# Read-back sums enter the PSUM banks by products with the identity at the end of a mixture of experts

## The chip, the cores and the metric

The kernel runs on one core of a Trainium2 chip. The metric is the device time of one execution in microseconds (us), as the median of several runs. The engines are TensorE (PE, with its weight loads shown apart as PEld), VectorE (DVE), ScalarE (ACT), GpSimd (POOL) and SyncE (SP, which issues most DMA transfers). TensorE writes into eight PSUM banks of 128 partitions by 512 f32 values.

## What is computed

A two-layer backbone block over 256 latent tokens and 256 context tokens of width 1024. Each layer mixes the tokens by four head groups, and then a mixture of 16 experts (two for each token) is added with a gate:

```python
def moe_ffn(h, w_router, router_bias, w_gate, w_up, w_down):
    ...
    y = jnp.zeros_like(h)
    for e in range(N_EXPERTS):
        a = jax.nn.silu(h @ w_gate[e]) * (h @ w_up[e])
        y = y + gates[..., e:e + 1] * (a @ w_down[e])
    return y
...
x = x_mid + g2 * moe_ffn(hf, ...)        # latent tokens
ctx = ctx_mid + cg2 * moe_ffn(hc, ...)   # context tokens, first layer only
```

So in the first layer 512 tokens, held as four tiles of 128 tokens by 1024, each receive gate vector times sum of expert outputs. After it the second layer starts with an RMSNorm of the same tiles.

## The kernel before

**Turns.** In the first layer `moe` runs 16 turns, one for each expert (`turn_0`, in the order `TURNS`). A turn gathers the expert's tokens in blocks of 64, multiplies them with the gate and up weights (`mm_in`, line 1544), forms silu times product with the token's weight (`act`, lines 1550 and 1551), transposes (`spin`, line 1557) and multiplies with the down weights (`mm_out`, line 1568). If the expert has more than 64 tokens, a second block runs in a branch (`If cv > BLK`), and inside it another branch (line 1760) covers a third block.

**Where the outputs go.** The first 15 experts add their rows to a table `sums` in device memory by indirect DMA (`put`, line 1451). At the end of turn 14 (`p == NE - 2`) the table is read back into four tiles `ACC` (line 1813); three of them lie over constants in the tile `cst`, which are loaded again later (line 531). In the same turn the gate vectors of latent and context tokens are spread over all partitions into `g2` (the tiles `G`). The last expert doesn't use the table. `parts` (lines 1586 on ACT and 1587 on DVE) splits each of its two output blocks into a rounded half and a rest, in `more` for the second block and `ST[0]` for the first, and `add` (line 1597) spreads them over the tokens by products with one-hot matrices, two such products for each bank, one bank for each half of a token tile. With `last` set DVE multiplies the bank by `g2` (line 1602), and DVE or POOL adds it to the residual tile `xres` (line 1603).

**The scaling before.** `scaled` multiplies each `ACC` tile by `g2` (line 1724) and adds it to `xres` (line 1725), tile 0 on DVE, tile 1's product on DVE and its sum on POOL, tiles 2 and 3 on POOL. It is called in the last turn between the first block's `act` and the second `mm_out`.

**Order.** Inside the turns PE, DVE and ACT execute in written order (a manual schedule). In the next layer's mixer (`mix(1)`) only PE's order is written out; a planner places the other engines' instructions, and it may put them into the end of the stage before: line 574, which computes the scale of the next layer's first norm, is an example. `stat` (lines 1840 and 1842, with 276 and 277) computes each tile's sum of squares for the next norm, whose first steps are lines 556 and 558 (DVE and ACT scale the tiles) and line 238 (PE transposes them).

**Banks.** `bank(tag)` takes a PSUM bank of a tag; there are one `tp`, one `md`, two `pj`, two `sc` and two `ob`. In the last turn `md` holds the second block's output and one `sc` the first block's.

**Matmul records.** An f32 product of 512 columns shows as two records in the trace, one whose operands are rounded to `fp32r` as one. The long convolution, whose rows stand below as a price, issues f32 products of 128x128 by 128x512:

```python
for f in (m, 2 + m):
    b = bank("sc")
    for tt in range(2):
        mm(b[:, :N], lhsT=C("df", tt * 512 + f * P, tt * 512 + (f + 1) * P),
           rhs=u[tt][:, :N], start=(tt == 0), stop=(tt == 1))
```

Of the kernel before, what the change touches and what calls it, by code (L numbers as in the profile page):

```python
# [14 lines left out]
OP = mybir.AluOpType  # L15
# [108 lines left out]
def hybrid_block_kernel(ctx: ExitStack, tc: tile.TileContext, xin, const, fconst, par, fpar, misc, fng,  # L124
                        ada, win, wout, exps, out, dump=None, upto=99):
    nc = tc.nc
# [10 lines left out]
    def bank(tag="tp"):  # L137
        return psp.tile([P, 512], F32, name="b_" + tag, tag=tag, bufs=BANKS[tag])
# [120 lines left out]
    def C(name, a=0, b=None):  # L259
        at, n = CONST[name]  # L260
        return cst[:, at + a:at + (n if b is None else b)]
# [5 lines left out]
    ident = C("ident")  # L267
# [100 lines left out]
    xres, norms = {}, []  # L368
# [1027 lines left out]
    def moe(l, cnt, idx, gc, pd, pk, rk, hx, h0, hp):  # L1396

        T = 4 if l == 0 else 2
        N = T * P
        S = N // L  # L1400
        V = nc.vector
        with ExitStack() as mctx:
            ep = mctx.enter_context(right(f"ep{l}"))
            ew = mctx.enter_context(right(f"ew{l}", 2))
            if l == 0:
# [5 lines left out]
                ACC = [cst[:, at + D * t:at + D * (t + 1)] for t in range(3)] + [ep.tile([P, D], F32, name="acc")]  # L1411
# [18 lines left out]
            b = bank()  # L1430
# [39 lines left out]
            if l == 0:  # L1470
# [7 lines left out]
                g2 = G  # L1478
# [100 lines left out]
            def parts(b, st):  # L1579

                if l:
                    V.tensor_mul(msc[:, :512], b, g2f)
                    b = msc[:, :512]
                for h in range(2):
                    a, o = slice(64 * h, 64 * h + 64), slice(64 - 64 * h, 128 - 64 * h)
                    nc.scalar.activation(st[h][a], b[a], AF.Copy)
                    V.tensor_tensor(st[h][o], b[a], st[h][a].bitcast(F32), op=OP.subtract)  # L1587
                return st

            def add(*blocks, only=None, last=False, banks=None):  # L1590

                for t in range(T) if only is None else only:
                    for h in range(2):
                        cs = slice(h * 512, (h + 1) * 512)
                        b = banks[h] if banks else bank("ob")
                        for i, (st, ohT) in enumerate(blocks):
                            nc.tensor.matmul(b, lhsT=ohT[:, t * P:(t + 1) * P], rhs=st[h],  # L1597
                                             start=(i == 0), stop=(i == len(blocks) - 1))
                        if last:
                            pool = h and t < T - 1  # L1600
                            y = AM[2] if pool and t % 2 == 0 else HE[1].rearrange("p k s -> p (k s)")[:, cs]
                            V.tensor_mul(y, b, g2[t // 2][:, cs])
                            (nc.gpsimd if pool else V).tensor_tensor(xres[t][:, cs], xres[t][:, cs], y, op=OP.add)
                        else:
                            y = xres[t] if l else ACC[t]
                            V.tensor_tensor(y[:, cs], b, y[:, cs], op=OP.add)  # L1606
# [70 lines left out]
            def turn_0(p, e, cv, w, b0):  # L1677

                start, last = p == 0, p == NE - 1
                h, nh = HE[p % 2], HE[(p + 1) % 2]  # L1680

                def prepare(q, part):

                    if q < NE:
                        turn(G[q % 2], 0, P, part=part, h=HE[q % 2])

                if start:
                    more = third()
                    b0 = mm_in(w, h0, between=lambda k: k > 2 and (next(more, None), next(more, None)))
                    b = bank("ob")  # L1690
# [5 lines left out]
                more = None, None  # L1696
                if last:
                    ST.append([ew.tile([P, 512], F32R, name=f"st{h}", tag="y") for h in range(2)])
                    owed = ST[0], OT[0]
                    more = ep.tile([P, 2, 512], F32R, name="stl", tag="HE0")  # L1700
                    more = [more[:, i] for i in range(2)]
# [3 lines left out]
                    more = more, OT[1]  # L1705
# [11 lines left out]
                    if not last:  # L1717
                        mm_in(nw, nh, b=b2, ks=ks)

                def scaled():  # L1720
                    if last:
                        for t in range(T):
                            eng = V if t == 0 else nc.gpsimd
                            (V if t < 2 else nc.gpsimd).tensor_tensor(ACC[t], ACC[t], g2[t // 2], op=OP.mult)
                            eng.tensor_tensor(xres[t], xres[t], ACC[t], op=OP.add)

                def first(steps):
                    if not start:
                        mm_in(w, h, b=b0, ks=range(HEAD, 8), between=lambda k: steps[k]() if k in steps else None)
                        act(b0, gc[:, 0, e:e + 1], AM[0])  # L1730
# [6 lines left out]
                def vector(c):  # L1737
                    if p == NE - 2:
                        for i in range(2):
                            nc.scalar.activation(g2[c][:, i * 512:(i + 1) * 512], bcast(mT[l][:, 5], i, c), AF.Copy)  # L1740

                with tc.If(cv > BLK, label=f"turn{p}") as branch:
                    tc.mark_branch_hint_location(f"third{p}", cv > P, engines=[ET.PE, ET.DVE, ET.Activation])
                    steps = {3: lambda: vector(0), 5: lambda: vector(1)}
                    b1 = mm_in(w, h[:, :, BLK:], tag="md", between=lambda k: steps[k]() if k in steps else None)
                    act(b1, gc[:, 1, e:e + 1], AM[1])
                    if last:
                        where(e, OT[1], C("slot", 1, 2))
                        where(e, OT[0], C("slot", 0, 1))
                    if start:  # L1750
                        spin(AM[1], AT[1])
                    first({4: lambda: spin(AM[1], AT[1])})
                    scaled()
                    steps = {1: lambda: prepare(p + 2, 0), 2: lambda: spin(AM[0], AT[0]),
                             3: lambda: (start and (prepare(1, 0), prepare(1, 1)), prepare(p + 2, 1))}
                    b1 = mm_out(w, AT[1], bank("md"), lambda f: steps[f]() if f in steps else None)
                    if last:
                        parts(b1, more[0])
                        mm_out(w, AT[0], out)
                        with tc.If(cv > P, label=f"third{p}"):  # L1760
                            add(more, last=True)
                            block(e, w, turn(X, 0, BLK, h=h0), g3[:, e:e + 1], C("slot", 2, 3), *temp, last=True)
                            with tc.If(cv > P + BLK):
                                overflow(e, w, cv, P + BLK, *temp, last=True)
                            zero(OT[1])
                        main.done(4)
                    else:
                        with tc.If(cv > P, label=f"third{p}") as branch2:
                            turn(X, 0, BLK, h=h0)
                            put(b1, rows[1][:, e:e + 1])  # L1770
                            b3 = mm_in(w, h0, tag="tp")
                            act(b3, g3[:, e:e + 1], AM[1])
                            head(0)
                            spin(AM[1], AT[1])
                            head(1)
                            put(mm_out(w, AT[1], bank("ob")), rows3[:, e:e + 1])
                            mm_out(w, AT[0], out)
                            with tc.If(cv > P + BLK):
                                overflow(e, w, cv, P + BLK, *temp)
                            main.done(4)  # L1780
                        with branch2.Else():
                            main.repeat()
                            put(b1, rows[1][:, e:e + 1])
                            head(0, 1)
                            mm_out(w, AT[0], out)
                with branch.Else():
                    first({4: lambda: vector(0), 6: lambda: vector(1)})
                    main.repeat()
                    if last:
                        where(e, OT[0], C("slot", 0, 1))  # L1790
                        where(e, OT[1], C("slot", 1, 2))
                    scaled()
                    if start:
                        spin(AM[0], AT[0])
                        mm_out(w, AT[0], out)
                        for q in (1, 2):
                            prepare(q, 0)
                            prepare(q, 1)
                        head(0, 1)
                    else:  # L1800
                        head(0)
                        prepare(p + 2, 0)
                        spin(AM[0], AT[0])
                        prepare(p + 2, 1)
                        head(1)
                        mm_out(w, AT[0], out)
# [11 lines left out]
                if not last:  # L1818
                    main.done(2)
                    return ncv, nw, b2  # L1820
                parts(out, ST[0])
                for t in range(T):
                    add(owed, more, only=[t], last=True)
                    if t:
                        stat(t - 1)
                stat(T - 1)
# [311 lines left out]
```

## Time and profile before

| | us |
|---|---|
| median of 3 runs | 1328.83 |
| lowest and highest | 1328.79 and 1328.98 |
| the profiled execution | 1331.17 |
| its span in the trace | 1329.1 |
| PE busy in the span | 1146.8 (86%) |
| DVE busy | 538.7 (41%) |
| ACT busy | 314.6 (24%) |
| POOL busy | 293.9 (22%) |

Busy shares are means over stages that have different limits; the stage of this change lies from about 795 to 830 us. Times in rows are microseconds from the start of the span unless ns is written. [...] A bracket with an arrow names how long the engine had been idle and what released it.

### The profile page before, as it was taken

How to read it: one execution, taken by the hardware profiler on the slowest of the kernel's cores; microseconds unless marked ns; L12 is line 12 of the kernel's file. 1: busy time of each engine (PE TensorE's matmuls, PEld its weight loads, DVE VectorE, ACT ScalarE, POOL GpSimd, SP SyncE). 2: the span in 40 equal slices, each digit the busy share in tenths (PEclk: the TensorE clock that was granted, in tenths of full speed). 3: DMA queues.
4: the chain of work that ended last, by engine and by line, in shares of the span. 5: the costliest groups of instructions: out<-in, count | busy, mean ns of one | idle time of the engine just before them, and what ended most of it. 6: DMA issues, size and time to landing. Idle time of an engine off the chain costs nothing. (4 is left out here: it accounts for less than half of the span.)

```text
span 1329.1 us, 16569 instructions
## 1 busy us (share of the span) xinstructions
PE 1146.8 (86%) x6205; PEld 644.2 (48%) x6205; DVE 538.7 (41%) x1070; ACT 314.6 (24%) x569; POOL 293.9 (22%) x238
## 2 busy tenths in 40 slices
PE   6799998888899789988898996878879699999995
PEld 2456565566588633323333333657669433343331
DVE  5431867325522641101011028496443535434444
ACT  2422233222312211111111114424333211111111
POOL 4432231322023312111112036543315000000000
PEclk9999998988789879989899996989869799998998
DMA  9485443412563689399999936120135399994971
GB/s 366 192 320 190 153 164 112 158 55 83 180 254 127 232 354 329 113 381 384 394 382 401 374 120 229 64 90 23 64 127 219 129 397 419 419 404 188 411 299 50
DMA packets 48559, 310.61 MB, mean 234 GB/s; under 512 B 6017, under 2 KB 6209, under 8 KB 14096
## 3 DMA queue, kind: packets, MB, share of 16 engines
q1 hardware_dynamic: 41936, 292.77, 56.4%
q0 software_dynamic: 6320, 15.27, 4.4%
q8 instruction: 91, 1.49, 0.4%
q14 instruction: 68, 0.56, 0.1%
q10 hardware_dynamic: 144, 0.52, 0.1%
HBM read 297.99 MB, written 12.32 MB: 233 GB/s over the span
## 5 line engine op out<-in xcount | busy, mean ns | idle before, releaser
L603 POOL TENSOR_TENSOR ws<-w,ws 128x1024 fp32r<-128x1024 f32 x50 | 121.3, 2439 | 218.2 <-ACT ws L602 200.8
L1544 PE MATMUL b_pj<-w,HE 128*64 128x512 f32 x416 | 107.6, 653 | 23.1 <-issue 20.8
L234 PE MATMUL b_pj<-hh,ws 128*128 128x512 f32 (+1 forms) x448 | 123.0, 364 | 1.1 <-POOL ws L603 1.1
L1568 PE MATMUL b_sc<-w,rows 128*64 128x512 f32 x448 | 103.7, 604 | 0.6 <-ACT rows L1558 0.6
L693 DVE SCALAR_TENSOR_TENSOR cacc<-gl,pr,cacc 128x512 f32<-128x512 f32 (+1 forms) x120 | 92.7, 772 | 2.6
L234 PEld LDWEIGHTS b_pj<-hh,ws 128*128 128x128 f32 x448 | 79.9, 199 | 21.0 <-issue 9.7
L234 PE MATMUL b_pj<-hl,ws 128*128 128x512 f32 (+1 forms) x224 | 78.8, 352 | 0.0
L1544 PEld LDWEIGHTS b_pj<-w,HE 128*64 128x64 f32 x416 | 34.1, 149 | 84.5 <-issue 82.3
L602 ACT ACTIVATE ws<-w 128x1024 fp32r<-128x1024 f32 x50 | 52.5, 1052 | 70.2 <-PE b_pj L234 44.6
L277 POOL TENSOR_TENSOR rf<-rf,half 128x1 f32<-128x1 f32 x2 | 1.1, 551 | 287.9 <-DVE rf L276 287.9
L1606 DVE TENSOR_TENSOR x<-b_ob,x 128x512 f32<-128x512 f32 x68 | 44.0, 687 | 43.4 <-PE b_ob L1597 43.3
L1451 POOL DMA_INDIRECT sums<-y,rws x19 | 29.8, 1566 | 135.6 <-DVE y L1450 116.4
L1568 PEld LDWEIGHTS b_sc<-w,rows 128*64 128x64 f32 x448 | 31.1, 138 | 58.3 <-issue 56.5
L1551 DVE SCALAR_TENSOR_TENSOR X<-X,gc,b_pj 64x512 f32<-64x512 f32 x16 | 12.1, 754 | 107.7 <-ACT X L1550 107.7
L234 PE MATMUL b_md<-w,sT 128*32 128x256 f32 x704 | 54.3, 434 | 1.3 <-DVE mT L313 1.3
L1544 PE MATMUL b_pj<-w,hf 128*64 128x512 f32 x224 | 53.9, 618 | 1.0 <-PEq L1920 0.6
L1544 PE MATMUL b_pj<-w,x 128*64 128x512 f32 x224 | 52.9, 601 | 1.0 <-PEq L1920 1.0
L1450 DVE COPY y<-b_sc 128x512 f32<-128x512 f32 x15 | 10.4, 692 | 96.5 <-PE b_sc L1568 50.3
L1597 PE MATMUL b_ob<-st,ohT 128*128 128x512 f32 x76 | 33.6, 511 | 16.6 <-DVE st L1587 9.9
L234 PEld LDWEIGHTS b_pj<-hl,ws 128*128 128x128 f32 x224 | 44.6, 199 | 5.4
L1550 ACT ACTIVATE X<-b_pj 64x512 f32<-64x512 f32 x16 | 9.4, 588 | 157.3 <-PE b_pj L1544 149.6
L1456 POOL DMA_INDIRECT G<-hbuf,idx x15 | 15.2, 1013 | 105.8 <-PE b_ob L1528 56.7
(475 smaller groups left out, 2062.8 us busy)
## 6 DMA issues: line engine op xcount, KB each, us to landing
w<-in_exps_dram SPq DMA_DIRECT2D x168, 1024.0 KB
w<-in_ada_dram SPq DMA_DIRECT2D x48, 1024.0 KB
w<-in_win_dram SPq DMA_DIRECT2D x16, 1024.0 KB
hold<-in_exps_dram SPq DMA_DIRECT2D x12, 1024.0 KB
w<-in_wout_dram SPq DMA_DIRECT2D x8, 1024.0 KB
hf<-in_exps_dram SPq DMA_DIRECT2D x6, 1024.0 KB
cst<-in_exps_dram SPq DMA_DIRECT2D x6, 1024.0 KB
pr<-in_par_dram SPq DMA_DIRECT2D x2, 1461.5 KB
```

The source lines that it names most:

```text
L234: nc.tensor.matmul(out_, lhsT=lhsT, rhs=rhs, **kw)
L602: nc.scalar.activation(wh[:, :n], src, AF.Copy)
L603: nc.gpsimd.tensor_tensor(wl[:, :n], src, wh[:, :n].bitcast(F32), op=OP.subtract)
L693: nc.vector.scalar_tensor_tensor(ac, gl[:, :, j:j + L], R("cvw", i * 31 + j, i * 31 + j + 1), ac, op0=OP.mult, op1=OP.add)
L1450: V.tensor_copy(y, b)
L1451: nc.gpsimd.indirect_dma_start(out=sums[:, :], out_offset=bass.IndirectOffsetOnAxis(ap=row, axis=0), in_=y, in_offset=None, bounds_check=1 ...
L1456: nc.gpsimd.indirect_dma_start(out=g, out_offset=None, in_=hbuf[:, :], in_offset=bass.IndirectOffsetOnAxis(ap=ix, axis=0), bounds_check=N ...
L1544: nc.tensor.matmul(b[64 * j:64 * j + 64], lhsT=x, rhs=w[k // 2][:, at:at + 512], start=(k == 0), stop=(k == 7), tile_position=(0, 64 * j))
L1551: V.scalar_tensor_tensor(a[64:], a[64:], gate[64:], b[64:], op0=OP.mult, op1=OP.mult)
L1568: nc.tensor.matmul(b[64 * j:64 * j + 64], lhsT=aT[:, f, :], rhs=w[4 + f // 2][:, at:at + 512], start=(f == 0), stop=(f == 3), tile_positio ...
L1597: nc.tensor.matmul(b, lhsT=ohT[:, t * P:(t + 1) * P], rhs=st[h], start=(i == 0), stop=(i == len(blocks) - 1))
L1606: V.tensor_tensor(y[:, cs], b, y[:, cs], op=OP.add)
```

## The change

The scaling and adding of the read-back sums (`scaled`, 8 operations) goes. Instead each bank of the last expert's sums is begun by a product of the identity with the matching half of `ACC`, which leaves the bank open, and the two one-hot products add to it; the existing multiplication by `g2` then scales both. Six of the eight banks are begun ahead of the first sum, in tags `ob`, `ob`, `pj`, `pj`, `sc`, `tp`; the last two, for tile 3, reuse the `ob` banks once DVE has read them.

```diff
-            def add(*blocks, only=None, last=False, banks=None):
+            def add(*blocks, only=None, last=False, banks=None, more=False):
...
                             nc.tensor.matmul(b, lhsT=ohT[:, t * P:(t + 1) * P], rhs=st[h],
-                                             start=(i == 0), stop=(i == len(blocks) - 1))
+                                             start=(i == 0 and not more), stop=(i == len(blocks) - 1))
...
-                def scaled():
-                    if last:
-                        for t in range(T):
-                            eng = V if t == 0 else nc.gpsimd
-                            (V if t < 2 else nc.gpsimd).tensor_tensor(ACC[t], ACC[t], g2[t // 2], op=OP.mult)
-                            eng.tensor_tensor(xres[t], xres[t], ACC[t], op=OP.add)
...
                     first({4: lambda: spin(AM[1], AT[1])})
-                    scaled()
...
                         where(e, OT[1], C("slot", 1, 2))
-                    scaled()
...
                 parts(out, ST[0])
+
+                def begun(i):
+
+                    b = bank(("ob", "ob", "pj", "pj", "sc", "tp", "ob", "ob")[i])
+                    nc.tensor.matmul(b, lhsT=ident, rhs=ACC[i // 2][:, i % 2 * 512:(i % 2 + 1) * 512], start=True, stop=False)
+                    return b
+
+                banks = [begun(i) for i in range(6)]
                 for t in range(T):
-                    add(owed, more, only=[t], last=True)
+                    add(owed, more, only=[t], last=True, banks=banks[2 * t:2 * t + 2] if t < 3 else [begun(6), begun(7)], more=True)
                     if t:
                         stat(t - 1)
                 stat(T - 1)
```

## Rows read from the trace of the kernel before

**Rows 1.** Windows: stretch, length, each engine's busy us (instructions), PEclk, DMA share, GB/s.
```profile
784.00:797.00 13.00, 11.16 (x56) 3.75 (x52) 4.61 (x6) 1.95 (x4) 5.91 (x7) 1.00 0.74 258
797.00:801.40 4.40, 4.31 (x22) 1.15 (x16) 4.37 (x3) 0.59 (x1) 4.40 (x2) 1.00 0.04 11
801.40:808.10 6.70, 0.00 (x0) 0.00 (x0) 5.25 (x7) 1.19 (x3) 6.70 (x4) 0.70 0.44 158
808.10:818.00 9.90, 8.66 (x16) 4.19 (x16) 8.95 (x16) 4.02 (x12) 6.26 (x10) 0.50 0.78 287
...
822.00:828.00 6.00, 5.76 (x24) 4.71 (x24) 4.09 (x10) 5.23 (x11) 0.62 (x1) 0.50 0.89 348
```
**Rows 2.** Timeline of PE: start, us, line, operation, tiles, shape, count.
```profile
787.57 0.50 PE L1575 MATMUL b_tp<-pdT,pick 16*128 16x512 f32 x1 [1.84 <-DVE ohT L1576]
...
797.71 3.60 PE L1568 MATMUL b_sc<-hold,rows 128*64 128x512 f32 x16
808.12 0.79 PE L1597 MATMUL b_ob<-st,ohT 128*128 128x512 f32 x1 [6.80 <-DVE st L1587]
808.71 0.63 PE L1597 MATMUL b_ob<-stl,ohT 128*128 128x512 f32 x1
...
821.85 0.45 PE L238 MATMUL b_pj<-cst,xs 128*128 128x128 f32 x1 [4.00 <-issue]
```
**Rows 3.** Timeline of DVE, with one row of ACT.
```profile
797.77 3.02 DVE L1724 TENSOR_TENSOR cst<-cst,G 128x1024 f32<-128x1024 f32 x1
...
802.69 0.59 ACT L1586 ACTIVATE st<-b_sc 64x512 fp32r<-64x512 f32 x1 [0.55 <-ACTq L1760]
803.59 3.76 DVE L574 SCALAR_TENSOR_TENSOR aT<-mT,msc 128x4 f32<-128x4 f32 x4 [0.72 <-DVEq L1760]
807.38 0.69 DVE L1587 TENSOR_TENSOR st<-b_sc,st 64x512 fp32r<-64x512 f32 x1
808.72 0.69 DVE L1587 TENSOR_TENSOR st<-b_sc,st 64x512 fp32r<-64x512 f32 x1 [0.66 <-ACT st L1586]
809.44 0.69 DVE L1602 TENSOR_TENSOR HE<-b_ob,G 128x512 f32<-128x512 f32 x1
...
819.11 0.69 DVE L1603 TENSOR_TENSOR x<-x,HE 128x512 f32<-128x512 f32 x1
```
**Rows 4.** Line 574, whole trace: count, ns min/median/max.
```profile
L574 DVE SCALAR_TENSOR_TENSOR aT<-mT,msc x8: 148/348/2301, 31.4 to 807.2; 128x4 f32<-128x4 f32 x8
```
**Rows 5.** Timeline of POOL, first and last of five operations back to back.
```profile
796.84 2.87 POOL L1724 TENSOR_TENSOR cst<-cst,G 128x1024 f32<-128x1024 f32 x1 [7.09 <-DMA cst<-sums]
...
807.22 2.00 POOL L1725 TENSOR_TENSOR x<-x,cst 128x1024 f32<-128x1024 f32 x1
```
**Rows 6.** Prices on PE at full clock: f32 products, then single records.
```profile
246.15 3.70 PE L234 MATMUL b_sc<-u,cst 128*128 128x512 f32 x8 [1.50 <-ACT p L841]
...
L234 PE MATMUL b_sc<-u,cst x16: 592/592/697, 246.1 to 257.7; 128*128 128x512 f32 x16
...
838.32 0.62 PE L234 MATMUL b_pj<-hh,ws 128*128 128x512 f32 x2
838.78 0.39 PE L234 MATMUL b_pj<-hl,ws 128*128 128x512 f32 x1
```
**Rows 7.** Last read-back DMA: issue by POOL, and us to landing.
```profile
788.69 1.07 POOL L1813 DMA_DIRECT2D acc<-sums  x1
...
acc<-sums POOLq DMA_DIRECT2D x1, 512.0 KB, 9.3
```
**Rows 8.** Line 1760: branch instructions, ns min/median/max, first and last start.
```profile
L1760 PEldq COMPARE_BRANCH  x2: 187/1818/3448, 796.9 to 801.5; - x2
L1760 ACTq COMPARE_BRANCH  x2: 38/48/59, 801.6 to 802.2; - x2
```
**Rows 9.** Windows of PE alone: stretch, length, busy us, PEclk, DMA share, GB/s.
```profile
804.00:805.00 1.00, 0.00 (x0) 0.57 0.95 401
828.00:830.00 2.00, 1.54 (x10) 0.99 0.71 270
```

## The prediction

> **What bounds the kernel now.** First the page's 40 slices show that TensorE (PE) is busy nearly everywhere and that the slices around 800 us are among its thinnest; so I read that stretch in windows by engine [rows 1]. Up to 801.4 us PE is full at a granted clock of 1.00. From 801.40 to 808.10 it executes nothing, while GpSimd (POOL) is full; from 808.10 to 818.00 DVE is busy 8.95 of 9.90 us. The reader is to see that one engine hands the end of this stage to the next: POOL and DVE first, then DVE, then the norm of the next layer. PE's timeline says the same in two brackets: it waited 6.80 us for line 1587 on DVE (the second half of the split of the expert's output) and 4.00 us at the start of the next layer [rows 2].
>
> Why is line 1587 late? The last records of the expert's second product start at 797.71 and last 3.60, so its bank is ready at 801.31 [rows 2]. On DVE stand, in order, the last scaling of the sums (3.02 us), the split of the other half, four tiny operations of the next layer's first step (3.76 us together) and only at 807.38 the first split of this bank [rows 3]. Those tiny operations take 148 ns at their shortest and 2301 ns at their longest [rows 4]; during all four POOL runs its scalings and additions, five back to back from 796.84 to 809.22 [rows 5]. So what delays PE is POOL's work, through DVE. Sums begin on PE at 808.12, the first multiplication of line 1602 at 809.44, the last addition ends at 819.80 and the next layer's first product starts at 821.85 [rows 2, 3].
>
> **What the change removes.** Eight whole-tile operations: three on DVE, the last of them 3.02 us, and five on POOL [rows 3, 5]. None goes off the path directly; what goes is their shadow. DVE is then free when line 1586 on ScalarE (ACT) has written its half of the first split, and the tiny operations cost 4 x 0.148 = 0.6 us [rows 4]. I follow the chain: bank at 801.31, ACT 0.59 to about 802.0, DVE 0.69 to 802.8, ACT 0.59, DVE 0.69 to about 804.2, durations and alternation as in [rows 3]. The split that PE waited for at 808.07 is thus ready some 5 us sooner, the second one at 804.2 instead of 809.41. DVE would gain 5.2 us if nothing else came.
>
> **What it adds.** Eight products with the identity, 128x128 by 128x512 in f32, on PE. Such a product leaves two records in the trace: the long convolution's code issues two products for each of two banks where the trace has 8 records. These 8 take 3.70 us, and one record alone 0.592 [rows 6], so (3.70 - 0.592) / 7 = 0.444 us a record, 0.888 a product; 3.70 / 4 = 0.925 is the upper end.
>
> [...]
>
> Six of the eight products stand in PE's order behind the expert's last product and ahead of the first sum. Their inputs have landed: the last read-back was issued at 788.69 and landed 9.3 us later, at 798.0 [rows 7]. Their banks are free: md, which still holds the other half, isn't used. So they start as soon as PE has passed the end of the branch. Its second branch instruction stands at 801.5 and lasts 0.19 [rows 8], that is to 801.69; how long until the first product, the trace of before doesn't show, as PE then waited for DVE. Nearest are ACT, 0.45 us from its second branch (802.2) to its next instruction (802.69), and DVE, idle 0.72 before its own [rows 3, 8]. I take ACT's, 802.15, with 801.69 and 802.40 as ends.
>
> The sum: 802.15 + 6 x 0.888 = 807.48 for the first sum product on PE. It and its fellow are single records that follow each other at 0.23 us at full clock, the last 0.39 long [rows 6], so the bank is ready at 808.10; 0.10 later (809.34 to 809.44 in before, [rows 2, 3]) DVE multiplies: **808.20 instead of 809.44, 1.24 us sooner**. With the ends: 801.69 + 5.33 gives 1.7 us, 802.40 + 5.55 gives 0.8 us. So most of the 5.2 us is taken by the identity products, which are now what is late: the splits wait for them some 3 us.
>
> From there DVE sets the pace as before: eight multiplications, five additions and small operations, 10.36 us from 809.44 to 819.80 [rows 3] almost without idle time (8.95 of 9.90, [rows 1]). Faster products on PE bring nothing in it. The seventh and eighth identity products wait for the ob banks that DVE frees after its first and third operation, about 810.3, and end near 812; the sums of the last tile follow by 813, and DVE comes to them at about 808.2 + 7.3 = 815.5, so 2.5 us cover them. POOL's L1603 additions and the norm remain. The reload of the constants under the read-back sums now waits for PE, near 807.5 rather than POOL's 809.2, and the expert loads behind it on SP's queue come that much sooner; nobody waits for them. Last, the next layer starts at half clock either way: PE now idles from 813 to about 820.6. From 822 to 828 PE is busy 5.76 of 6.00 us at 0.50, and the clock is back in the window that starts at 828 [rows 1, 9]. I take the return at the same distance from the restart; 2 us more or fewer at half clock of a full PE are 1 us of time, either way. So the forecast is -1.24 us, its own range -2.2 to -0.2.
>
> The profiled execution spans 1329.1 us and took 1331.17; the median of the runs is 1328.83. The difference is applied to the median: 1328.83 - 1.24 = **1327.6 us**.
>
> **The rivals.**
> *The products run at half clock (slower).* In before the clock fell at about 804.15 (0.57 of the window from 804), 2.8 us after PE stopped [rows 9]. If it also falls in the new stretch, a product costs 1.78 us: 802.15 + 10.7 = 812.8, first multiplication at about 813.9, 4.5 us later than before, and the last two products (3.6 us) then reach DVE too, some 1 us: about 1334. It decides from the point at which the gap of 0.84 us in front of the products is enough for the fall. Against it: a gap of 1.84 us at 785.7 left the clock at 1.00 [rows 1, 2]. Chance 0.05.
>
> *The clock is given back earlier.* Full clock through the restart would spare up to half of the 5.76 busy us of 822 to 828, 2.9 us, hence 1324.7. For it: PE works full in the old gap. Against: it idles longer just before the restart, 7.6 instead of 4.0 us. Chance 0.10.
> [...]
>
> *PE isn't the limit.* If the identity products were out of the way by the time the splits are done (they ran ahead of the branch's end, or cost a single 0.23 each), DVE would begin at 804.2, 5.2 us sooner: 1323.6. PE executes them in written order and its records speak for 0.888. Chance 0.04.
>
> *The next layer is put in another order.* Outside this stage only PE's order is the written one; the four tiny operations of line 574, which belong to the next layer and stand inside this one [rows 3], show a planner at work on DVE. With POOL and DVE free at other times it may order DVE, ACT and POOL differently. As a price I take the largest wait of PE in before's new layer that follows, 4.0 us [rows 2], halved, in either direction: 1325.6 to 1329.6. Chance 0.11.
>
> **How the numbers follow.** Forecast 0.70. A measurement of this kernel can tell about 0.2%, 2.7 us, from no change, so the forecast counts as "same", though three runs lie within 0.2 us of each other. Faster: 0.10 + 0.04 and a little of the reordering, 0.16; slower 0.05 and a little, 0.07; same 0.77. The range reaches to the earlier clock's nearer half and the reordering's ends, 1325.0 to 1329.4.
>
> **What would show it.** Right: no scaling on DVE and POOL at 795 to 809; splits done by about 804.5; six identity products back to back from about 802.2 with a granted clock of 1.00, 0.89 us each; the first L1602 near 808.2, DVE full for 10.4 us, next layer near 820.6. Wrong: a clock below 1.00 between 802 and 808; DVE idle for less than 2 us before the first multiplication; another order on DVE behind 820; a first identity product later than 802.5.

## The result: slower by about 1%

| | median us | lowest to highest | runs |
|---|---|---|---|
| before | 1329.76 | 1328.79 to 1340.04 | 13 |
| changed | 1346.35 | 1340.58 to 1350.80 | 13 |

The ratio of changed to before is 1.0096, 95% interval 1.0076 to 1.0115, that is 10 to 15 us more. Forecast were 1327.6 us, a change too small for a measurement to tell. The profiled execution of the changed kernel took 1346.71 us and spans 1344.6.

Single executions of one kernel differ by 10 to 16 us here (the kernel before took 1328.79 to 1340.04 beside the changed one and 1327.18 to 1342.80 beside later runs), more than the prediction assumed from its three runs. So besides each ratio I use a length inside one profile: from the moment when the last expert's bank is ready (end of the `b_sc` records of line 1568) to the next layer's first product (line 238). Before, that is 821.85 - 801.31 = 20.54 us [rows 2].

TensorE's timeline of the changed kernel; columns as in [rows 2], line 1817 is the identity product, counts are records:
```profile
802.33 3.60 PE L1568 MATMUL b_sc<-hold,rows 128*64 128x512 f32 x16
816.38 3.58 PE L1817 MATMUL b_ob<-cst 128*128 128x512 f32 x4 [10.44 <-DMA cst<-sums]
820.05 1.99 PE L1817 MATMUL b_pj<-cst 128*128 128x512 f32 x4
823.81 1.12 PE L1817 MATMUL b_sc<-cst 128*128 128x512 f32 x2 [1.78 <-DMA cst<-sums]
824.78 1.02 PE L1817 MATMUL b_tp<-cst 128*128 128x512 f32 x2
825.24 0.79 PE L1597 MATMUL b_ob<-st,ohT 128*128 128x512 f32 x1
...
838.61 0.45 PE L238 MATMUL b_pj<-cst,xs 128*128 128x128 f32 x1 [7.40 <-issue]
```
The bank is ready at 805.93, the first identity product starts 10.45 us later, and the bracket names what it waited for: the transfer of the read-back sums. A second wait of 1.78 us has the same cause. The length is 838.61 - 805.93 = 32.68 us, 12.14 more than before, which is about the loss in whole runs. VectorE's timeline shows that the splits weren't late:
```profile
806.07 2.44 DVE L574 SCALAR_TENSOR_TENSOR aT<-mT,msc 128x4 f32<-128x4 f32 x4 [0.81 <-PEq L1752]
808.55 0.69 DVE L1587 TENSOR_TENSOR st<-b_sc,st 64x512 fp32r<-64x512 f32 x1
809.89 0.69 DVE L1587 TENSOR_TENSOR st<-b_sc,st 64x512 fp32r<-64x512 f32 x1 [0.66 <-ACT st L1586]
826.30 0.69 DVE L1602 TENSOR_TENSOR HE<-b_ob,G 128x512 f32<-128x512 f32 x1 [15.71 <-PE b_ob L1597]
```
They are done at 810.58, and then VectorE sits for 15.71 us. Why the transfers were late stands in the timelines of GpSimd (line 1804 is the read-back, line 1813 before), ScalarE and SyncE:
```profile
784.94 1.55 POOL L1451 DMA_INDIRECT sums<-y,rws  x1 [7.52 <-issue]
785.96 2.91 POOL L603 TENSOR_TENSOR ws<-w,ws 128x1024 fp32r<-128x1024 f32 x1
805.94 2.34 POOL L603 TENSOR_TENSOR ws<-w,ws 128x1024 fp32r<-128x1024 f32 x1 [17.07 <-ACT ws L602]
808.22 1.75 POOL L1804 DMA_DIRECT2D cst<-sums  x3
809.96 0.53 POOL L1804 DMA_DIRECT2D acc<-sums  x1
...
804.81 1.06 ACT L602 ACTIVATE ws<-w 128x1024 fp32r<-128x1024 f32 x1 [0.27 <-ACTq L1752]
...
808.73 1.63 SPq L183 DMA_DIRECT2D w<-in_exps_dram  x3
```
Before, the four transfers were issued from 786.95 on, 14.4 us ahead of the bank, and line 602 had executed twice by then (GpSimd and ScalarE):
```profile
782.34 5.21 POOL L603 TENSOR_TENSOR ws<-w,ws 128x1024 fp32r<-128x1024 f32 x2
786.95 2.28 POOL L1813 DMA_DIRECT2D cst<-sums  x3
...
775.24 1.99 ACT L602 ACTIVATE ws<-w 128x1024 fp32r<-128x1024 f32 x2
```
Now they are issued from 808.22 on, 2.3 us behind the bank. Ahead of them in GpSimd's order stands the second of two operations of the next layer (line 603, the rest of a weight piece after rounding), which waited 17.07 us for its partner on ScalarE (line 602, the rounding), and that one executes only when ScalarE has left the last turn's branch.

The branch instructions of the profiles show the order. The inner branch of the last turn, behind the place where `scaled` stood, has line 1760 before and line 1752 in the changed kernel; first GpSimd before, then GpSimd and ScalarE in the changed kernel (columns as in [rows 8]):
```profile
L1760 POOLq COMPARE_BRANCH  x2: 38/42/45, 803.1 to 810.6; - x2
...
L1752 POOLq COMPARE_BRANCH  x2: 38/42/45, 782.3 to 783.8; - x2
...
L1752 ACTq COMPARE_BRANCH  x2: 38/48/59, 804.0 to 804.6; - x2
```
On GpSimd before, line 603 twice and the read-back are ahead of it (803.1); in the changed kernel GpSimd is past it at 783.8, and the last indirect write (784.94), line 603 twice and the read-back come behind it. On ScalarE before, both roundings of line 602 are done by 777.2, long ahead of the branch (801.6 [rows 8]); in the changed kernel the second, at 804.81, comes behind it. In the written program the read-back is at the end of turn 14 in both.

### The profile page after: what moved, and what is told of

Its sections match the earlier page's. It is cut to its first block, busy times and chain, and to the rows that moved or that the text cites. A ratio compares the mean times of both kernels' runs of the same rounds, so it can differ in the third digit from the quotient of the medians.

```text
span 1344.6 us, 16593 instructions
## 1 busy us (share of the span) xinstructions
PE 1154.3 (86%) x6221; PEld 645.9 (48%) x6221; DVE 531.3 (40%) x1067; ACT 314.7 (23%) x569; POOL 281.6 (21%) x233
## 5 line engine op out<-in xcount | busy, mean ns | idle before, releaser
L1544 PE MATMUL b_pj<-w,HE 128*64 128x512 f32 x416 | 112.6, 678 | 23.3 <-issue 16.4
L1586 ACT ACTIVATE st<-msc 64x512 fp32r<-64x512 f32 x34 | 21.4, 628 | 70.4 <-DVE msc L1582 70.0
L1597 PE MATMUL b_ob<-st,ohT 128*128 128x512 f32 x72 | 30.3, 493 | 8.4 <-DVEq L1907 5.1
```

Of the source, the lines that this page charges most:

```text
L1544: nc.tensor.matmul(b[64 * j:64 * j + 64], lhsT=x, rhs=w[k // 2][:, at:at + 512], start=(k == 0), stop=(k == 7), tile_position=(0, 64 * j))
```

## The theories

**A.** The loss is the late issue of the read-back. The branch used to contain its user (`scaled`), so whatever orders GpSimd's instructions had to issue the transfers ahead of the branch. The change moved the user behind the branch, and GpSimd, whose order in the turns isn't the written one, put the transfers behind it too.
**B.** The loss is in the identity products: their price, or the clock.

## Experiments

**One user back in the branch.** `reach()` is called in both arms where `scaled()` stood:
```diff
+                def reach():
+                    if last:
+                        seen = ew.tile([P, 4], F32, name="seen", bufs=1)
+                        for t in range(T):
+                            nc.gpsimd.tensor_copy(seen[:, t:t + 1], ACC[t][:, :1])
```


> The changed kernel plus four one-column copies of the read-back tiles on GpSimd, in both arms of the last turn's branch where the scaling stood; nobody reads what they write. They give the branch a user of the sums, so that the four read-back transfers stand ahead of the branch in GpSimd's order again. Theory A (the loss is the read-back's late issue: in the changed kernel it was issued at 808.2 us, behind the branch, where before issued it at 786.95): issue returns to 787-792 us, TensorE's waits of 10.4 and 1.8 us for the sums go, and the time is that of the prediction, 0 to 2 us below before. Theory B (the identity products themselves, by clock or price, cost the time): at least 8 us above before stay.

Measured: ratio 1.000 (0.998 to 1.002), median 1333.38 beside 1333.03 for before on that chip. The loss is gone. GpSimd's and TensorE's timelines of this kernel (line 1812 is the read-back, 1825 the identity product):
```profile
792.72 2.28 POOL L1812 DMA_DIRECT2D cst<-sums  x3
794.46 1.06 POOL L1812 DMA_DIRECT2D acc<-sums  x1
...
804.95 3.60 PE L1568 MATMUL b_sc<-hold,rows 128*64 128x512 f32 x16
809.21 1.96 PE L1825 MATMUL b_ob<-cst 128*128 128x512 f32 x4 [0.66 <-DVE aT L574]
811.01 1.88 PE L1825 MATMUL b_pj<-cst 128*128 128x512 f32 x4
812.73 1.02 PE L1825 MATMUL b_sc<-cst 128*128 128x512 f32 x2
813.59 1.02 PE L1825 MATMUL b_tp<-cst 128*128 128x512 f32 x2
814.05 0.80 PE L1597 MATMUL b_ob<-st,ohT 128*128 128x512 f32 x1
...
827.46 0.45 PE L238 MATMUL b_pj<-cst,xs 128*128 128x128 f32 x1 [7.41 <-issue]
```
The read-back is 15.8 us ahead of the bank (808.55), TensorE waits 0.66 us, and the length is 18.91 us: 1.63 less than before. The ratio alone couldn't tell that from nothing.

**The wait alone taken away.** The identity products read the gate tile instead of the sums, so the sums of 15 experts are left out of the result:
```diff
-...lhsT=ident, rhs=ACC[i // 2][:, i % 2 * 512:(i % 2 + 1) * 512], start=True, stop=False)
+...lhsT=ident, rhs=G[0][:, i % 2 * 512:(i % 2 + 1) * 512], start=True, stop=False)
```


> The changed kernel with the identity products reading the gate tile G instead of the read-back sums, so that they wait for no transfer; the sums of the first 15 experts are left out of the result, the transfers stay and are still issued late. Theory A: 0 to 2 us below before, the products start within 1 us of the end of the expert's last product. Theory B: 8 us or more above before.

Measured: ratio 0.9989 (0.9964 to 1.0014), length 18.76 us, although the read-back is still issued at 803.20, 2.3 us behind the bank (800.89):
```profile
801.45 1.96 PE L1817 MATMUL b_ob<-G,cst 128*128 128x512 f32 x4 [0.55 <-PEq L1752]
...
803.20 1.74 POOL L1804 DMA_DIRECT2D cst<-sums  x3
```
By the starts of the first, third, fifth and sixth (801.45, 803.24, 804.96 and 805.82) the products take 0.86 to 0.90 us each, forecast were 0.888; B falls.

**No identity product, but the user behind the branch.** The kernel before with its scaling moved:
```diff
-                    scaled()
...
-                    scaled()
...
+                scaled()
                 parts(out, ST[0])
```


> The kernel before with its scaling called behind the branch, ahead of the splits, and no identity product at all. Theory A (the planner puts the read-back behind a branch that doesn't use it): the transfers are issued behind 800 us, and the kernel is slower than before by 12 us or more, as the whole scaling follows them. Theory B: within 7 us of before, since the scaling alone takes that long behind the branch.

Measured: ratio 1.0154 (1.0118 to 1.0190), length 37.52 us, 17 more than before. GpSimd's timeline (line 1811 is the read-back):
```profile
799.36 2.34 POOL L603 TENSOR_TENSOR ws<-w,ws 128x1024 fp32r<-128x1024 f32 x1 [14.08 <-ACT ws L602]
801.65 1.75 POOL L1811 DMA_DIRECT2D cst<-sums  x3
803.39 0.53 POOL L1811 DMA_DIRECT2D acc<-sums  x1
815.51 2.00 POOL L1724 TENSOR_TENSOR cst<-cst,G 128x1024 f32<-128x1024 f32 x1 [11.59 <-DMA cst<-sums]
```
The same order and the same wait arise without any identity product. What moves the transfers is where their user stands.

**The changed kernel again**, on the chip of the runs that follow.

> The changed kernel once more, beside the runs that follow on the same chip. Both theories: 8 to 14 us above before; a second profile shows whether the parts of the loss are the same: read-back issued behind 800 us, TensorE waiting 10 to 12 us for it, and any remaining difference ahead of the last turn's branch as a lower granted clock there.

Measured: ratio 1.0070 (1.0047 to 1.0093), length 33.37 us, of which 11.13 us are the first wait for the sums. The issue is again 2.3 us behind the bank.

**GpSimd in written order**, and nothing else:
```diff
-                with tc.manual_schedule(engines={ET.PE, ET.DVE, ET.Activation}):
+                with tc.manual_schedule(engines={ET.PE, ET.DVE, ET.Activation, ET.Pool}):
```


> The changed kernel with GpSimd among the engines whose order in the turns is the written one, and nothing else. The read-back transfers then stand ahead of the branch again without a user in it. Theory A (late issue by the planner's order): issue near 787-792 us, no wait of TensorE for the sums, the stage from the expert's last product to the next layer's first one 18.5 to 19.5 us (before 20.5, changed kernel 32.7, with the four copies 18.9), time 0 to 2 us below before. If the order of other GpSimd work suffers: above before.

Measured: ratio 0.9986 (0.9964 to 1.0009), length 18.89 us, read-back 18.3 us ahead of the bank (801.70):
```profile
783.43 2.29 POOL L1804 DMA_DIRECT2D cst<-sums  x3
```
The order is enough; no user in the branch is needed.

**What holds the read-back behind the branch?** GpSimd passed it early (783.8 above), and the indirect write at 784.94 stands behind it too. So line 603 should be the holder. Here the two operations of line 603 that stand ahead of the read-back go to VectorE:
```diff
-                nc.gpsimd.tensor_tensor(wl[:, :n], src, wh[:, :n].bitcast(F32), op=OP.subtract)
+                eng = nc.vector if l and len(pieces) <= 2 else nc.gpsimd
+                eng.tensor_tensor(wl[:, :n], src, wh[:, :n].bitcast(F32), op=OP.subtract)
```


> The changed kernel with the second half of the splitting of the next layer's first two weight pieces (line 603) on VectorE instead of GpSimd; the read-back stays behind the branch in GpSimd's order, but no longer behind line 603. Two theories of what holds it: A1, line 603, which waited 17.1 us for ScalarE's line 602 behind the branch: issue 10 us or more before the end of the expert's last product, no wait of TensorE for the sums, 0 to 2 us below before (two operations of about 1 us on VectorE lie in its 3.8 us of waiting). A2, the end of the branch itself: issue stays behind the expert's last product, 6 us or more above before.

Measured: ratio 0.9992 (0.9970 to 1.0015), length 18.93 us. GpSimd's timeline (lines are 4 further down):
```profile
790.96 1.55 POOL L1455 DMA_INDIRECT sums<-y,rws  x1 [7.50 <-issue]
796.14 1.72 POOL L1808 DMA_DIRECT2D cst<-sums  x3 [3.63 <-DMA sums<-y,rws]
797.86 0.53 POOL L1808 DMA_DIRECT2D acc<-sums  x1
```
The read-back is behind the branch in the program and still issued 12.7 us ahead of the bank; it waits for the last write of the sums and for nothing else. So the branch itself costs GpSimd no such time. The holder was line 603, and behind it ScalarE's order. Why the planner put the second rounding behind ScalarE's branch, no run shows.

**The identity products just ahead of their sums**, first with the four copies, then with GpSimd in written order:
```diff
-                banks = [begun(i) for i in range(6)]
+                banks = [begun(i) for i in range(2)]
                 for t in range(T):
-                    add(..., banks=banks[2 * t:2 * t + 2] if t < 3 else [begun(6), begun(7)], more=True)
+                    add(..., banks=banks, more=True)
+                    if t < T - 1:
+                        banks = [begun(2 * t + 2), begun(2 * t + 3)]
```


> The same, with the identity products of a tile just ahead of that tile's sums, two at a time, instead of six ahead of all. Theory A with the prediction's working (the splits are ready at about 804.2 us and wait for six products of 0.888 us): the first multiplication comes 3.5 us earlier than with six ahead, TensorE then needs 2.7 us a tile where VectorE needs 2.6, so the stage ends 2.5 to 3.5 us earlier: some 4 us below before. If VectorE's start isn't set by the six products: the same time as with six ahead.

> GpSimd in written order, and the identity products just ahead of their tile's sums: the version that should beat both. Stage of 15.5 to 16.5 us as with the four copies and this order (15.9), 3 to 5 us below before. If the four copies had done something else than moving the transfers: above that.

Measured: ratio 0.9977 (0.9958 to 0.9995) with the copies, 0.9944 (0.9923 to 0.9965) in written order, length 15.90 us in both. VectorE's timeline of the second, whose bank is ready at 803.41:
```profile
805.52 0.69 DVE L1587 TENSOR_TENSOR st<-b_sc,st 64x512 fp32r<-64x512 f32 x1 [0.66 <-ACT st L1586]
806.54 0.69 DVE L1602 TENSOR_TENSOR HE<-b_ob,G 128x512 f32<-128x512 f32 x1 [0.33 <-PE b_ob L1597]
...
809.22 0.69 DVE L1602 TENSOR_TENSOR HE<-b_pj,G 128x512 f32<-128x512 f32 x1 [0.67 <-PE b_pj L1597]
...
811.88 0.69 DVE L1602 TENSOR_TENSOR HE<-b_sc,G 128x512 f32<-128x512 f32 x1 [0.38 <-PE b_sc L1597]
```
The first multiplication comes 3.13 us after the bank (8.13 before, 6.56 with six products ahead), now right behind the splits, and TensorE is just behind VectorE's pace: 0.3 to 0.7 us of waiting at each tile. This is the version that beats both kernels, the one before by 4.64 us of length. The two ratios differ by 0.33%, with intervals that overlap only from 0.9958 to 0.9965, while the lengths are equal; why the second lies lower in whole runs, by more than the 3 to 5 us expected, stays open.

All of it in one table (us; each from its profile):

| kernel | read-back issue, from the bank | bank to first identity product | bank to first multiplication | bank to next layer | ratio |
|---|---|---|---|---|---|
| before | -14.4 | | 8.13 | 20.54 | 1 |
| changed | +2.3 | 10.45 | 20.37 | 32.68 | 1.0096 |
| changed, again | +2.3 | 11.13 | 21.07 | 33.37 | 1.0070 |
| user in the branch | -15.8 | 0.66 | 6.56 | 18.91 | 1.0000 |
| products read no sums | +2.3 | 0.56 | 6.45 | 18.76 | 0.9989 |
| before, user behind | +2.3 | | 21.30 | 37.52 | 1.0154 |
| GpSimd in written order | -18.3 | 0.67 | 6.56 | 18.89 | 0.9986 |
| line 603's two on VectorE | -12.7 | 0.66 | 6.56 | 18.93 | 0.9992 |
| just ahead, with copies | -14.3 | 0.66 | 3.12 | 15.90 | 0.9977 |
| just ahead, written order | -15.4 | 0.67 | 3.13 | 15.90 | 0.9944 |

## Why the prediction was wrong

**The step that failed** is "Their inputs have landed: the last read-back was issued at 788.69 and landed 9.3 us later, at 798.0" [rows 7]. That time was carried over from before, as if an instruction that the diff doesn't touch kept its place. In the turns only TensorE, VectorE and ScalarE are in written order; GpSimd isn't among them, as the description of the kernel says. (Even on those three, instructions of the next layer can move, as line 602 did on ScalarE.) The scaling that the change removed was the reason for the place: it needed the sums inside the branch. The changed kernel waits 10.45 us there instead of 0.84, and another 1.78 at the third tile; both waits are gone when the read-back is ahead again, be it by a user in the branch, by GpSimd's written order or by moving line 603.

**The rival that came nearest** named the planner at work, but looked for its effect only behind the stage, in the next layer, and priced it at 2 us either way. The evidence used for it, line 574 inside this stage, should have raised the question for GpSimd's queue inside the stage: what keeps the read-back where it is? A moved user was counted with its own operations; the transfers that serve it weren't.

**What held**, in the kernels with the order restored:
- *The shadow.* With only four memsets of 0.11 to 0.12 us on GpSimd beside them the four operations of line 574 take 0.38 us (forecast 0.6, before 3.76 [rows 3]). In the changed kernel they take 2.44, beside line 603 on GpSimd. The second split is done 2.80 us after the bank with the user in the branch (810.66 + 0.69 - 808.55); forecast were 2.9.
- *The products.* They start 0.66 us after the bank (forecast 0.84, ends 0.38 and 1.09), at 0.86 to 0.90 each (0.888). The first multiplication comes 6.56 us after the bank, forecast 6.89.
- *VectorE sets the pace.* With the user in the branch it goes from 815.11 to 825.41, 10.30 us (10.36). The next layer starts 18.9 us after the bank, forecast 20.54 - 1.24 = 19.30. The gain of this part was under-sized: 1.63 us, not 1.24.
- *The splits wait for six products.* With two ahead instead of six the first multiplication comes 3.43 us earlier, as the "some 3 us" had it.

**The clock.** The rival of products at half clock did happen, as a consequence: in the changed kernel the first four records take 820.05 - 816.38 = 3.67 us where the kernel with the user in the branch needs 1.80, after TensorE had been idle for 10.44 us. TensorE's windows show it, changed kernel first and then the one with the user in the branch (columns as in [rows 9]; PEclk is the share of its full speed that TensorE was granted):
```profile
816.00:820.00 4.00, 3.58 (x4) 0.54 1.02 428
820.00:826.00 6.00, 4.17 (x10) 1.00 0.82 337
...
809.20:814.00 4.80, 4.79 (x11) 1.00 0.88 326
```
This slowness adds nothing to the loss. TensorE's weight loads waited for the sums again ahead of the second tile's products (to 820.05) and of the third's (to 823.81), so faster products would only have waited longer (who waited for what, us in total, times, longest):
```profile
PEld b_sc L1817 <- DMA cst<-sums: 2.6, 1, 2.6
...
PEld b_pj L1817 <- DMA cst<-sums: 1.5, 1, 1.5
```
My argument against that rival was weak, though: "a gap of 1.84 us at 785.7 left the clock at 1.00" [rows 1, 2]. A gap of 1.83 or 1.84 us stands there in all these profiles, and in three the clock was lower in or behind it: 0.50 from 789 to 794 in the changed kernel, 0.75 from 793 to 797 with the user in the branch, 0.57 from 784 to 789 with GpSimd in order. In the kernels with the order restored the gap in front of the products was 0.66 or 0.67 us. They ran at 1.00 with the user in the branch (809.2 to 814) and with the products just ahead in written order (803 to 816); in the other three the first four records take the same 1.96 us as in these two.

## What to carry to other kernels

When a change moves the user of a transfer, ask of every engine whose order a planner makes what held the issue where it was, and look up the new order of that queue before any time of the old trace is carried over. A transfer that was early because a branch needed it can become late when nothing in the branch does, and in its queue it can then stand behind an unrelated operation that waits for a third engine. Where the place matters, write it down (a manual order), and put work that others wait for just ahead of its use rather than all of it first.

## What the runs showed that I had not expected

The clock's response to a short gap differs between executions. Windows at the 1.84 us gap in front of the same work, of different lengths; columns as in [rows 9], first before (gap from 785.73), then the changed kernel (from 787.24), then GpSimd in order (from 783.03):
```profile
788.00:793.00 5.00, 5.00 (x27) 1.00 0.88 310
...
790.00:794.00 4.00, 4.00 (x12) 0.50 0.00 0
...
784.00:789.00 5.00, 4.14 (x9) 0.57 0.79 269
```
From the one-hot product behind the gap (the second of line 1575) to the bank it takes 13.73 or 13.74 us in seven of the ten profiles, in before's at a mean granted clock of 1.00, and the eight records that follow take 1.94 us in each of the seven. It takes 15.31, 16.85 and 16.84 us in three, with the user in the branch, in the changed kernel (at a mean granted clock of 0.80) and with GpSimd in order; there the eight records take 2.40, 3.68 and 3.68 us. The second profile of the changed kernel is among the seven, so the kernel doesn't decide it. So some 3 us of the difference between the two first profiles (4.6 us at the bank) aren't the change's, and single profiles are compared by lengths inside a stage here. Whether this explains the whole spread of 10 to 16 us between executions was not tried.

The late transfers were also slower where the next weights were loaded beside them. In the second profile of the changed kernel, where the expert weights (three of 1 MB) are issued at the same time, the first three transfers of the read-back took 11.8 us in the median and the last one 16.1, against 7.9 and 9.3 [rows 7] before:
```profile
w<-in_exps_dram SPq DMA_DIRECT2D x3, 1024.0 KB, 12.0
cst<-sums POOLq DMA_DIRECT2D x3, 512.0 KB, 11.8
...
acc<-sums POOLq DMA_DIRECT2D x1, 512.0 KB, 16.1
```
The run whose products read no sums takes the overlap away: its read-back is just as late (803.20), but its expert weights are issued only at 813.84, and it landed nearly as fast as before, 8.3 us for the first three in the median and 9.7 for the last:
```profile
cst<-sums POOLq DMA_DIRECT2D x3, 512.0 KB, 8.3
acc<-sums POOLq DMA_DIRECT2D x1, 512.0 KB, 9.7
```
That speaks for the weights' traffic as the cause; no run moved the weights alone.
